# Two-layer hybrid trunk on one core: one more pair of feed-forward tiles with held weights, the normalised product one slot later, the last norm's sums one product later

## The chip, the cores and the metric

One core of a Trainium2 chip. The metric is the device time of one execution in microseconds. TensorE (PE) multiplies, VectorE (DVE) and ScalarE (ACT) work on what it leaves in PSUM and prepare its operands in SBUF, and the queue of SyncE (SP) issues nearly all DMAs. GpSimd (POOL) does next to nothing here.

## The reference

Input and output are 256 tokens by 1024 channels in float32. Layer 0 mixes tokens by a short gated convolution, layer 1 by block-sparse causal attention (with 256 tokens it is causal attention in one block, 16 heads of 64, rotary positions). After each comes the feed-forward that the change is about:

```python
def rmsnorm(x, g):
    var = jnp.mean(x * x, axis=-1, keepdims=True)
    return (x * lax.rsqrt(var + RMS_EPS)) * g

def conv_ffn(h, w_up, w_conv, w_down):          # w_up 1024 x 5632, w_down 2816 x 1024
    gu = causal_dwconv(h @ w_up, w_conv)        # three taps along the tokens
    g, u = jnp.split(gu, 2, axis=-1)
    return (jax.nn.silu(g) * u) @ w_down

for i in range(2):
    x = x + mixer_i(rmsnorm(x, mix_norm[i]))
    x = x + conv_ffn(rmsnorm(x, ffn_norm[i]), ffn_w_up[i], ffn_w_conv[i], ffn_w_down[i])
return rmsnorm(x, final_norm)
```

## The kernel before

**Numbers in two parts.** Every operand of PE is split into a high part `hi` (or `h`) and a rest `lo` (`l`), and a product is three matmuls: high by high, high by low, low by high. All weights come from HBM once, as 204 units of 128x1024, two units to a DMA of 1 MB (`raw<-wall`), four such buffers. For each unit ACT writes `hi<-raw` and DVE `lo<-raw,hi`. There are six buffers of each, so a unit is split up to six units before PE uses it.

**Order.** Each engine is wrapped in `InOrder`: it runs its instructions in the order in which the program writes them, and an instruction that waits holds back all behind it. `PLAN` lists the units in the order in which PE uses them. After each unit's matmuls `slot()` splits one more unit and then moves every task in `tasks` on by one piece; the tasks are Python generators, started by `spawn`, each `yield` ending a piece. So "a slot" is the time of one unit on PE.

**A feed-forward, `ffn(layer, ...)`.** 2816 features are 22 tiles of 128, each with a gate half and an up half. Tiles 2c and 2c+1 are pair c. A pair is computed in one of two ways.

- Pairs in `TURNED[layer]` go *wide*: four units `W c.kk` of 12 matmuls each, in which the input x is loaded as the stationary operand and the weights stream by, 512 columns at a time. The result lies by tokens in two PSUM banks (`w0_8_0` is layer 0, pair 8, tokens 0 to 127) and has to be turned. `crossed` does that: two DVE `STREAM_TRANSPOSE` into a buffer, then 16 small DMAs on SP's queue into a second buffer. The two buffers are both called `flip` in layer 0; in layer 1 the first is `vts` and the second `late`. `SETTLE` counts the slots from there until the task `whole` takes tile 2c (`SETTLE - 5` slots) and tile 2c+1 (one more). It also sets when `ffn_steps` thinks the tile ready to be used.
- The others go with *held weights*, by `narrow`: one unit per half and tile, the weights as the stationary operand, 8 times a matmul of 512 and one of 256 columns. The result lies by features; `gathered` adds its two parts (an ACT copy and a DVE add for each half).

`whole` then makes a tile into an operand: the product `gn` with 1/rms (`rstd`, DVE, 128x512), the three taps (`gy`: two ACT, four DVE instructions), silu (`s`, ACT), the product with the up half (`p`, DVE) and its split into `ps..h` (ACT) and `ps..l` (DVE). `ps_18l` in the profile is the low part of tile 18 (of either layer).

A *down* step `D j` multiplies tile j by its unit of `w_down` into accumulators `fo` (24 matmuls of 256 columns in layer 0, 12 of 512 in layer 1, where the result lies by tokens). `ffn_steps` puts a down step behind every second up step as soon as a tile is ready; the rest stand at the end, by readiness. The last two downs (layer 0) or three (layer 1) are done column by column in `acc.finish`, so that what follows can start early.

With the numbers of before, the end of layer 0's feed-forward is, in PE's order: W8.2 W8.3 D10 W9.0 W9.1 D11 W9.2 W9.3 D12, tile 20, D13, tile 21, D14 D15 D16 D17 D20 D18, and at the end D19 with D21. In layer 1: W9.0 W9.1 D12 W9.2 W9.3 D13, tile 20, D14, tile 21, D15 D16 D17 D20, and at the end D18, D19, D21.

**The norm.** The up-projection starts before the norm's sum is known, and 1/rms is applied to its result. `finish_norm` sums the squares over features by two matmuls with ones (`ss<-totalh`, `ss<-totall`) into a PSUM bank, ACT takes the square root (`rms`), DVE the reciprocal. `n` counts the steps of the loop in `ffn`; in layer 1 the first two (tile 0) are done ahead of the loop, so that n = 0 is the third product.

Of the kernel before, what the change touches and what calls it, by code (L numbers as in the profile page):

```python
# [55 lines left out]
FIRST += [(k, tuple((j, i) for j in range(2) for i in range(3))) for k in range(HALVED, ND)]  # L56


TURNED = {0: range(10), 1: range(1, 10)}
SETTLE = 6  # L60


def ffn_steps(layer):

    ups = []
    for c in range(NF // 2):
        if c in TURNED[layer]:
            ups += [("wide", layer, c, kk) for kk in range(4)]
# [3 lines left out]
    for i, key in enumerate(ups):  # L72
        steps.append(key)
        n += 1
        if key[0] == "wide" and key[3] == 3:
            ready.update({2 * key[2] + j: n + SETTLE + 5 + j for j in range(2)})
        elif key[:3] == ("up", layer, 1):
# [31 lines left out]
INDEX = {k: i for i, k in enumerate(PLAN)}  # L109
# [57 lines left out]
def trunk(ctx: ExitStack, tc: tile.TileContext, x, wall, small, ropes, masks, final, out):  # L167
# [21 lines left out]
    def line(pool, w, off=0, dtype=F32, **kw):  # L189

        return pool.tile([P, -(-(off + w) // LINE) * LINE], dtype, **kw)[:, off : off + w]
# [8 lines left out]
    def by_place(v):  # L200
        return v.rearrange("p (i a) -> p a i", a=2)
# [85 lines left out]
    def spawn(*gens):  # L287
        tasks.extend(gens)

    def slot(splits=1, ahead=True, order=None):  # L290

        def place(g):
            name = g.__name__
            if order:
                return (*order, name).index(name)
            return 2 * (name not in ("copied", "gathered")) + ((name == "rotate") == ahead)

        for _ in range(splits if ahead else 0):
            split_next()
        for g in sorted(tasks, key=place):  # L300
            if next(g, StopIteration) is StopIteration:
                tasks.remove(g)
        for _ in range(0 if ahead else splits):
            split_next()
# [83 lines left out]
    def table(func):  # L388

        t = line(ap_, 1, name="table", tag="table", bufs=1)  # L390
        S.activation(t, ones[:, 0:1], func)
# [186 lines left out]
    def split_act(h, l, v):  # L578
        S.activation(h, v, AF.Copy)
        V.tensor_sub(l, v, h.bitcast(F32))  # L580

    def half_tile(name):
        return ap_.tile([P, T], F32, name=name, tag="t", bufs=NT)

    def pair_tile(name):
        return ap_.tile([P, 2, T], F32, name=name, tag="big", bufs=NBIG)

    def split_turned(name, v):

        h, l = (turned(name=name + c, tag="ps" + c, bufs=NPS) for c in "hl")  # L590
        split_act(h.places, l.places, by_place(v))
        return h.columns, l.columns
# [175 lines left out]
    def ffn(layer, nm, i, then, turns):  # L768
        acc, ps = (TokenAccum if then is None else Accum)(f"fo{layer}"), {}
        gus = {}  # L770
        tag = "ab"[then is not None]

        gns = {}

        def gathered(j, h):

            t = gns[j][:, h, :].rearrange("p (a i) -> p a i", a=2)
            S.activation(t, by_place(gus[j][h][:, 1, :]), AF.Copy)
            V.tensor_add(t, by_place(gus[j][h][:, 0, :]), t)
            yield  # L780

        def whole(j, src=None, wait=0):
            for _ in range(wait):
                yield
            y = pair_tile(f"gy{layer}_{j}")
            s, p = half_tile(f"s{layer}_{j}"), half_tile(f"p{layer}_{j}")
            if src is None:
                gn = gns.pop(j)
                V.tensor_mul(gn, gn, nm.r[:, None, :].to_broadcast([P, 2, T]))
            else:  # L790
                gn = pair_tile(f"gn{layer}_{j}")
                V.tensor_mul(
                    gn.rearrange("p h (b i) -> p h b i", i=32),
                    src,
                    nm.r.rearrange("p (b i) -> p b i", i=32)[:, None].to_broadcast([P, 2, 8, 32]),
                )
            yield
            taps(*((y[:, h, :], gn[:, h, :], partial(ffn_tap, layer, half=h, j=j)) for h in range(2)))
            yield
            S.activation(s, y[:, 0, :], AF.Silu)  # L800
            V.tensor_mul(p, s, y[:, 1, :])
            yield
            if layer == 0:
                ps[j] = split_turned(f"ps{layer}_{j}", p)
                return
            ps[j] = split_tiles(f"ps{layer}_{j}", f"down{layer}")
            split_act(*ps[j], p)

        def crossed(c, banks):

            there, back = (v[c % 2] for v in turns)
            for t in range(2):
                V.transpose(there[:, t], banks[t])
            dst = back.rearrange("p (t b f) -> p t b f", t=2, b=4)
            for b in range(4):
                for q in range(4):
                    Q.dma_start(
                        dst[32 * q : 32 * q + 32, :, b],
                        there[32 * b : 32 * b + 32, :, q * P : (q + 1) * P],
                    )  # L820
                yield
            src = back.rearrange("p (b j h i) -> p j h b i", j=2, h=2, i=32)
            spawn(*(whole(2 * c + j, src[:, j], SETTLE - 5 + j) for j in range(2)))

        def wide(c, kk):
            if kk == 0:
                gus[c] = [
                    bank(f"w{layer}_{c}_{t}", tag=tag).rearrange("p a t -> p (a t)") for t in range(2)
                ]
            wh, wl = (  # L830
                w.rearrange("p (k a i) -> p k i a", k=2, a=2) for w in unit(("wide", layer, c, kk))
            )
            for k2 in range(2):
                k = 2 * kk + k2
                s = (slice(None), k2)
                for t in range(2):
                    xh, xl = (x_[:, t * P : (t + 1) * P] for x_ in nm.plain[k])
                    kw = {"skip_group_check": True}
                    E.matmul(gus[c][t], xh, wh[s], start=k == 0, stop=False, **kw)
                    E.matmul(gus[c][t], xl, wh[s], start=False, stop=False, **kw)  # L840
                    E.matmul(gus[c][t], xh, wl[s], start=False, stop=k == 7, **kw)
            if kk == 3:
                spawn(crossed(c, gus.pop(c)))

        def narrow(h, j):
            gu = bank(f"gu{layer}_{j}_{h}", tag=tag)
            if h == 0:
                gns[j] = pair_tile(f"gn{layer}_{j}")
                gus[j] = []
            gus[j].append(gu)  # L850
            project_both(gu, unit(("up", layer, h, j)), nm)
            spawn(gathered(j, h))
            if h and j:
                spawn(whole(j))

        steps = ffn_steps(layer)
        if ("up", layer, 0, 0) in steps:
            gus[0] = [bank(f"gu{layer}_0_{h}", tag=tag) for h in range(2)]
            gns[0] = pair_tile(f"gn{layer}_0")
            wg, wu = unit(("up", layer, 0, 0)), unit(("up", layer, 1, 0))  # L860
            for ks in ((0, 1), (2, 3), (4, 5), (6, 7)):
                project_both(gus[0][0], wg, nm, ks)
                project_both(gus[0][1], wu, nm, ks)
            spawn(gathered(0, 0), gathered(0, 1))
            steps = steps[2:]
            if then is None:
                spawn(turn(acc))
            slot(ahead=layer == 0)
            slot(ahead=layer == 0)
        else:  # L870
            assert then is not None
        last = 2 + (then is None)
        downs = [key for key in steps if key[0] == "down"]
        final = downs[-last:]
        for n, key in enumerate(steps[:-last]):
            if key[0] == "wide":
                wide(*key[2:])
            elif key[0] == "up":
                narrow(*key[2:])
            else:  # L880
                acc.add(key, ps[key[2]], key == downs[0], False)
            if layer == 0 and n == 4:
                Q.dma_start(rope, ropes)
                S.dma_start(mk, masks)
            if n == (2 if key[0] == "wide" and layer == 0 else 0):
                finish_norm(i, nm, tag=tag, ps=acc.b[3] if layer == 0 else None)
                if ("up", layer, 1, 0) in INDEX:
                    spawn(whole(0))
            if n == (3 if layer == 0 else 1):
                table(AF.Silu)  # L890
            slot(ahead=layer == 0 or n > 3 * LAG_FFN)
        while tasks:
            slot(0)
        table(AF.Sqrt)
        acc.finish(final, [ps[key[2]] for key in final], then)
# [451 lines left out]
```

## Time and profile before

| | |
|---|---|
| runs | 562.41, 562.59, 560.62 us (median 562.41) |
| profiled execution | 558.52 us, of which the span 556.7 |
| mean granted PE clock | 0.993 |
| busy of the span | PE 97%, DVE 89%, ACT 65% |
| chain that ended last | PE 88%, DVE 7%, DMA 2%, ACT 1%, issue 1% |
| transposes | 20 `flip<-w` and 18 `vts<-w` on DVE |
| small DMAs of `crossed` | 160 `flip<-flip` and 144 `late<-vts` of 32 KB, 3.4 us from issue to landing |
| wide matmuls | 608 `w<-hi,x` and 304 `w<-lo,x` of 512 columns, 379 ns |
| held matmuls | 96 `gu<-x,hi` of 512, 383 ns; 96 `gu<-x,lo` of 256, 273 ns |

Matmuls overlap: a matmul of 512 columns starts 0.22 us after the one before it, one of 256 columns 0.11, though each takes longer from start to end. A row of the timeline gives start, duration, engine, line, operation, what it writes and reads without buffer numbers, shapes, and in brackets for how long the engine was idle before it and what ended that. All lines are L150, the helper through which every instruction goes, so places are told apart by tiles and times.

### The profile page before, as it was taken

To read this page: it belongs to the slowest core of one execution; us is meant where nothing else is said; L and a number is where in the kernel's file an instruction comes from. 1 tells how busy PE (TensorE), PEld (TensorE's weight loads), DVE (VectorE), ACT (ScalarE), POOL (GpSimd) and SP (SyncE) were. 2 spreads that over 40 slices of the span, in tenths; PEclk is the share of its full clock that TensorE was granted. 3 is DMA by queue.
4 is the path that set the end of the run, shared out by engine and by line. 5 is a ranking of instruction groups with operands and counts; after the bars stand their busy time and mean duration, and the time that the engine had idled before them with its cause. 6 is when DMAs were issued, how large, how long until landed. Compare 5 with 4: busy or idle time off the path is not lost.

```text
span 556.7 us, 9269 instructions
## 1 busy us (share of the span) xinstructions
PE 540.9 (97%) x3319; PEld 491.0 (88%) x3319; DVE 496.9 (89%) x865; ACT 362.0 (65%) x628; POOL 7.9 (1%) x12
## 2 busy tenths in 40 slices
PE   9999999999999999996999999999999999999976
PEld 9999999888999999996989888898888888888965
DVE  6899998879988989999899999799969899999993
ACT  7656667555656656677757888876745566656654
POOL 0021010000000000000000000000000000000000
PEclk9999999999999999999999999999999999999998
DMA  8956774566767776765353444564757766666501
GB/s 278 380 191 227 258 266 152 208 195 215 233 230 239 253 259 239 247 231 184 121 214 154 152 152 164 215 226 153 272 189 244 275 244 220 235 240 238 187 3 75
DMA packets 43645, 117.76 MB, mean 212 GB/s; under 512 B 7120, under 2 KB 30032, under 8 KB 31568
## 3 DMA queue, kind: packets, MB, share of 16 engines
q1 hardware_dynamic: 43024, 116.44, 60.2%
q10 hardware_dynamic: 576, 0.74, 0.4%
q8 instruction: 26, 0.43, 0.3%
q14 instruction: 19, 0.16, 0.1%
HBM read 105.09 MB, written 1.05 MB: 191 GB/s over the span
## 4 chain that ended last, share of the span: by engine, by line
PE 88%; DVE 7%; DMA 2%; ACT 1%; issue 1%; SPq 0%; DVEq 0%; ACTq 0%
PE w L150 35%; PE fo L150 20%; PE v L150 6%; PE gu L150 4%; PE q L150 4%; PE mo L150 4%; PE k L150 4%; PE b L150 3%; DVE lo L150 3%; DMA raw<-wall 2%; PE cv L150 2%; PE c L150 2%; DVE gy L150 1%; PE s L150 1%; PE o L150 1%
## 5 line engine op out<-in xcount | busy, mean ns | idle before, releaser
L150 DVE TENSOR_TENSOR lo<-raw,hi 128x1024 fp32r<-128x1024 f32 (+3 forms) x204 | 239.6, 1187 | 15.5 <-ACT hi L150 14.7
L150 ACT ACTIVATE hi<-raw 128x1024 fp32r<-128x1024 f32 (+1 forms) x202 | 202.7, 1023 | 27.9 <-PE w L150 13.0
L150 PE MATMUL w<-hi,x 128*128 128x512 f32 x608 | 180.9, 379 | 0.0
L150 PEld LDWEIGHTS w<-hi,x 128*128 128x128 f32 x608 | 113.8, 189 | 15.5
L150 PE MATMUL w<-lo,x 128*128 128x512 f32 x304 | 115.2, 379 | 0.0
L150 DVE SCALAR_TENSOR_TENSOR gy<-gn,sm,gy 128x254 f32<-128x254 f32 (+1 forms) x176 | 73.1, 480 | 0.0
L150 ACT ACTIVATE gy<-gn,sm 128x256 f32<-128x256 f32 x88 | 39.8, 501 | 49.1 <-DVE gn L150 48.9
L150 PEld LDWEIGHTS w<-lo,x 128*128 128x128 f32 x304 | 57.5, 189 | 8.2
L150 ACT ACTIVATE s<-gy 128x256 f32<-128x256 f32 x44 | 18.3, 417 | 37.7 <-DVE gy L150 37.7
L150 PE MATMUL gu<-x,hi 128*128 128x512 f32 x96 | 31.9, 383 | 0.0
L150 PE MATMUL gu<-x,lo 128*128 128x256 f32 x96 | 26.2, 273 | 0.0
L150 PE MATMUL b<-x,hi 128*128 128x256 f32 (+1 forms) x96 | 25.2, 313 | 0.0
L150 DVE TENSOR_TENSOR gn<-flip,rstd 128x512 f32<-128x512 f32 x20 | 13.8, 689 | 12.4 <-DMA flip<-flip 11.9
L150 PE MATMUL cv<-x,hi 128*128 128x256 f32 x128 | 23.3, 281 | 0.0
L150 DVE TENSOR_TENSOR gn<-late,rstd 128x512 f32<-128x512 f32 x18 | 12.4, 690 | 11.1 <-DMA late<-vts 11.1
L150 PE MATMUL q<-x,hi 128*128 128x512 f32 x64 | 21.8, 389 | 0.0
L150 PE MATMUL ao<-ohl,hi 128*128 128x512 f32 x64 | 21.3, 385 | 0.0
L150 PE MATMUL k<-x,hi 128*128 128x512 f32 x64 | 21.2, 382 | 0.0
L150 PEld LDWEIGHTS gu<-x,hi 128*128 128x128 f32 x96 | 18.1, 189 | 2.6
L150 PEld LDWEIGHTS cv<-x,hi 128*128 128x128 f32 x128 | 20.0, 196 | 0.0
L150 PE MATMUL v<-hi,x 128*128 128x512 f32 x64 | 19.2, 382 | 0.0
L150 DVE TENSOR_TENSOR p<-s,gy 128x256 f32<-128x256 f32 x44 | 18.5, 421 | 0.0
(525 smaller groups left out, 1167.7 us busy)
## 6 DMA issues: line engine op xcount, KB each, us to landing
raw<-wall SPq DMA_DIRECT2D x94, 1024.0 KB, 5.3
flip<-flip SPq DMA_DIRECT2D x160, 32.0 KB, 3.4
late<-vts SPq DMA_DIRECT2D x144, 32.0 KB, 3.4
raw<-wall SPq DMA_DIRECT2D x9, 192.0 KB, 4.1
raw<-wall SPq DMA_DIRECT2D x3, 384.0 KB, 6.0
raw<-wall SPq DMA_DIRECT2D x2, 512.0 KB, 8.7
late<-vts SPq DMA_DIRECT2D x16, 64.0 KB, 2.0
out<-of SPq DMA_DIRECT2D x3, 256.0 KB, 2.1
```

The source lines that it names most:

```text
L150: r = f(*args, **kw)
```

## The change

```diff
 FIRST += [(k, tuple((j, i) for j in range(2) for i in range(3))) for k in range(HALVED, ND)]
 
 
-TURNED = {0: range(10), 1: range(1, 10)}
-SETTLE = 6
+TURNED = {0: range(9), 1: range(1, 9)}
+SETTLE = 7
 
 
...
@@ -850,8 +850,6 @@
             gus[j].append(gu)
             project_both(gu, unit(("up", layer, h, j)), nm)
             spawn(gathered(j, h))
-            if h and j:
-                spawn(whole(j))
 
         steps = ffn_steps(layer)
         if ("up", layer, 0, 0) in steps:
@@ -867,8 +865,6 @@
                 spawn(turn(acc))
             slot(ahead=layer == 0)
             slot(ahead=layer == 0)
-        else:
-            assert then is not None
         last = 2 + (then is None)
         downs = [key for key in steps if key[0] == "down"]
         final = downs[-last:]
@@ -882,12 +878,14 @@
             if layer == 0 and n == 4:
                 Q.dma_start(rope, ropes)
                 S.dma_start(mk, masks)
-            if n == (2 if key[0] == "wide" and layer == 0 else 0):
+            if n == 2 - layer:
                 finish_norm(i, nm, tag=tag, ps=acc.b[3] if layer == 0 else None)
-                if ("up", layer, 1, 0) in INDEX:
+                if layer == 1:
                     spawn(whole(0))
-            if n == (3 if layer == 0 else 1):
+            if n == 3 - 2 * layer:
                 table(AF.Silu)
+            if key[:3] == ("up", layer, 1):
+                spawn(whole(key[3]))
             slot(ahead=layer == 0 or n > 3 * LAG_FFN)
         while tasks:
             slot(0)

```

Pair 9 (tiles 18 and 19) leaves `TURNED` in both layers and goes with held weights. `SETTLE` starts `whole` of the remaining wide pairs one slot later. For held tiles `whole` is now started in the loop, ahead of that step's slot, as it was from `narrow`. `finish_norm` in layer 1 moves from the third product to the fourth (n = 0 to n = 1), and the spawn of tile 0 with it; in layer 0 it stays at n = 2. `table(AF.Silu)`, which loads ACT's table, stays at n = 3 and n = 1. Layer 0's branch without a held first tile loses an assertion only.

The end of layer 0's feed-forward becomes W8.2 W8.3 D10, tile 18, D11, tile 19, D12, tile 20, D13, tile 21, D14 D15 D18 D16 D17 D19, and at the end D20 with D21. In layer 1: D11, tile 18, D12, tile 19, D13, tile 20, D14, tile 21, D15 D18 D16 D17, and at the end D19, D20, D21.

Three places in the order of instructions follow; names carry the layer and the tile, then a running number of the buffer (`gn0_14` is layer 0's tile 14; `w0_8_0` pair 8).

DVE in layer 0 around the transposes of wide pair 8; `gn0_14` and `gn0_15` are the products of pair 7, `lo91` and on are weight splits. Before:

```order
L150 TENSOR_TENSOR lo90_2584<-raw42_2401,hi90_2583 128x1024
L150 TENSOR_TENSOR gn0_14_2590<-flip_1270,rstd1_1327 128x512
L150 STREAM_TRANSPOSE flip_1270<-w0_8_0_2461 128x512
L150 STREAM_TRANSPOSE flip_1270<-w0_8_1_2462 128x512
L150 TENSOR_TENSOR lo91_2623<-raw42_2401,hi91_2622 128x1024
L150 SCALAR_TENSOR_TENSOR gy0_14_2587<-gn0_14_2590,sm_71,gy0_14_2587 128x255 x2
L150 SCALAR_TENSOR_TENSOR gy0_14_2587<-gn0_14_2590,sm_71,gy0_14_2587 128x254 x2
L150 TENSOR_TENSOR gn0_15_2635<-flip_1270,rstd1_1327 128x512
L150 TENSOR_TENSOR lo92_2658<-raw43_2475,hi92_2657 128x1024
L150 TENSOR_TENSOR p0_14_2589<-s0_14_2588,gy0_14_2587 128x256
```

And now:

```order
L150 TENSOR_TENSOR lo90_2584<-raw42_2401,hi90_2583 128x1024
L150 STREAM_TRANSPOSE flip_1270<-w0_8_0_2450 128x512
L150 STREAM_TRANSPOSE flip_1270<-w0_8_1_2451 128x512
L150 TENSOR_TENSOR lo91_2618<-raw42_2401,hi91_2617 128x1024
L150 TENSOR_TENSOR gn0_14_2624<-flip_1270,rstd1_1327 128x512
L150 TENSOR_TENSOR lo92_2651<-raw43_2464,hi92_2650 128x1024
L150 TENSOR_TENSOR gn0_18_2631<-gu0_18_0_2630,gn0_18_2631 128x256
L150 SCALAR_TENSOR_TENSOR gy0_14_2621<-gn0_14_2624,sm_71,gy0_14_2621 128x255 x2
L150 SCALAR_TENSOR_TENSOR gy0_14_2621<-gn0_14_2624,sm_71,gy0_14_2621 128x254 x2
L150 TENSOR_TENSOR gn0_15_2665<-flip_1270,rstd1_1327 128x512
```

The product of tile 14 stood ahead of the transposes of pair 8 and now stands behind them and one split; between the products of tiles 14 and 15 there is now the add that gathers the gate half of tile 18.

DVE in layer 0 where tile 18 is finished. Before, near the end:

```order
L150 TENSOR_TENSOR p0_18_2993<-s0_18_2992,gy0_18_2991 128x256
L150 SCALAR_TENSOR_TENSOR gy0_19_3034<-gn0_19_3037,sm_71,gy0_19_3034 128x255 x2
L150 SCALAR_TENSOR_TENSOR gy0_19_3034<-gn0_19_3037,sm_71,gy0_19_3034 128x254 x2
L150 TENSOR_TENSOR p0_21_2998<-s0_21_2997,gy0_21_2996 128x256
L150 TENSOR_TENSOR lo105_3110<-raw49_2839,hi105_3109 128x1024
L150 TENSOR_TENSOR ps0_18l_3114<-p0_18_2993,ps0_18h_3113 128x256
L150 TENSOR_TENSOR p0_19_3036<-s0_19_3035,gy0_19_3034 128x256
L150 TENSOR_TENSOR ps0_21l_3120<-p0_21_2998,ps0_21h_3119 128x256
```

And now, ahead of the product of tile 16:

```order
L150 TENSOR_TENSOR p0_18_2708<-s0_18_2707,gy0_18_2706 128x256
L150 TENSOR_TENSOR lo96_2802<-raw45_2581,hi96_2801 128x1024
L150 TENSOR_TENSOR gn0_19_2753<-gu0_19_1_2782,gn0_19_2753 128x256
L150 TENSOR_TENSOR ps0_18l_2808<-p0_18_2708,ps0_18h_2807 128x256
L150 TENSOR_TENSOR gn0_19_2753<-gn0_19_2753,rstd1_1327 128x512
L150 TENSOR_TENSOR lo97_2840<-raw45_2581,hi97_2839 128x1024
L150 TENSOR_TENSOR gn0_16_2846<-flip_1270,rstd1_1327 128x512
```

The split of tile 18 (`ps0_18l`) was the third last of the feed-forward's DVE work; it now stands 38 rows ahead of the last, before the products of the last wide pair (`gn0_16` and 17).

PE in layer 1 around the sums of the last norm, `ss3`; `gu1_1_0` and `gu1_1_1` are the gate and up halves of tile 1. Before:

```order
L150 MATMUL gu1_1_0_4588<-x3_7_4501,hi140_4421 128x512
L150 MATMUL gu1_1_0_4588<-x3_7_4501,lo140_4422 128x256
L150 MATMUL ss3_4606<-totalh3_4520,ones_r_76 128x256
L150 MATMUL ss3_4606<-totall3_4521,ones_r_76 128x256
L150 MATMUL gu1_1_1_4633<-x3_0_4334,hi141_4447 128x512
L150 MATMUL gu1_1_1_4633<-x3_0_4334,lo141_4448 128x256
```

And now:

```order
L150 MATMUL gu1_1_1_4630<-x3_7_4509,hi141_4455 128x512
L150 MATMUL gu1_1_1_4630<-x3_7_4509,lo141_4456 128x256
L150 MATMUL ss3_4647<-totalh3_4528,ones_r_76 128x256
L150 MATMUL ss3_4647<-totall3_4529,ones_r_76 128x256
L150 MATMUL w1_1_0_4670<-hi142_4484,x3_0_4342 128x512 x2
L150 MATMUL w1_1_0_4670<-lo142_4485,x3_0_4342 128x512
L150 MATMUL w1_1_1_4671<-hi142_4484,x3_0_4342 128x512 x2
L150 MATMUL w1_1_1_4671<-lo142_4485,x3_0_4342 128x512
```

The two sums stood between the halves of tile 1 and stand now between its up half and the first wide pair, `w1_1`.

## The prediction

> **What bounds the kernel now.** I read the page's first section, then the chain of work that ended last, then the waits. The page:
>
> ```profile
> span 556.7 us, 9269 instructions
> PE 540.9 (97%) x3319; PEld 491.0 (88%) x3319; DVE 496.9 (89%) x865; ACT 362.0 (65%) x628; POOL 7.9 (1%) x12
> ```
>
> PE is busy for 97% of the span, so a gain must come from the few microseconds in which it waits or runs slowly. The profiled execution took 558.52 us, of which 1.8 lie around the span; the median of the runs, 562.41, is 3.9 above it. I make the sum in the profiled execution and take it off the median. About 0.5% (2.8 us) is what a measurement of this kernel can tell from no change.
>
> The chain, in order of time, around the ends of the two feed-forwards (start, us, what):
>
> ```profile
> 211.41 2.68 PE fo L150 x24
> 214.09 5.18 PE w L150 x24
> ...
> 229.81 5.24 PE gu L150 x32
> ...
> 242.97 13.41 PE fo L150 x120
> ...
> 256.92 1.13 DVE lo L150
> ...
> 261.35 0.43 DVE ps_18l L150
> ...
> 261.82 9.75 PE fo L150 x71
> ...
> 539.86 1.58 DVE gy L150 x4
> ```
>
> A down-projection (24 `fo` matmuls) costs 2.68 us, half a wide pair 5.18, a held tile 5.24. From 242.97 five downs run without a pause; then the chain leaves PE for DVE until `ps_18l`, the low half of tile 18's product. The waits (total, times, longest) and PE's own rows at both places say the same:
>
> ```profile
> PE fo L150 <- ACT ps_18h L150: 4.9, 2, 2.5
> PE fo L150 <- DVE ps_18l L150: 3.9, 2, 2.5
> DVE gn L150 <- DMA flip<-flip: 11.9, 8, 2.7
> DVE gn L150 <- DMA late<-vts: 11.1, 7, 3.6
> ```
>
> ```profile
> 256.09 0.28 PE L150 MATMUL fo<-ps_20h,lo 128*128 128x256 f32 x1
> 258.91 0.38 PE L150 MATMUL fo<-ps_18h,hi 128*128 128x256 f32 x1 [2.54 <-ACT ps_18h L150]
> 261.82 0.58 PE L150 MATMUL fo<-ps_18l,hi 128*128 128x256 f32 x1 [2.54 <-DVE ps_18l L150]
> ```
>
> ```profile
> 537.62 0.38 PE L150 MATMUL fo<-lo,ps_20h 128*128 128x512 f32 x1
> ...
> 540.36 0.48 PE L150 MATMUL fo<-hi,ps_18h 128*128 128x512 f32 x1 [2.36 <-ACT ps_18h L150]
> 542.16 0.79 PE L150 MATMUL fo<-hi,ps_18l 128*128 128x512 f32 x1 [1.32 <-DVE ps_18l L150]
> ...
> 545.16 0.38 PE L150 MATMUL fo<-lo,ps_19h 128*128 128x512 f32 x1
> ```
>
> PE is then slow for some 3 us. The clock by stretches (length, PE busy, granted clock, DMA share, GB/s), the last one around a short pause that comes up below:
>
> ```profile
> 542.00:543.00 1.00, 0.84 (x2) 0.50 0.00 0
> ...
> 545.00:546.00 1.00, 1.00 (x6) 0.99 0.00 0
> ...
> 381.00:382.20 1.20, 0.94 (x5) 1.00 0.92 389
> ```
>
> DVE is why tile 18 is late. Its rows in the first feed-forward:
>
> ```profile
> 217.56 0.69 DVE L150 TENSOR_TENSOR gn<-flip,rstd 128x512 f32<-128x512 f32 x1 [0.87 <-DMA flip<-flip]
> 218.16 1.31 DVE L150 STREAM_TRANSPOSE flip<-w 128x512 f32<-128x512 f32 x2
> ...
> 232.80 0.69 DVE L150 TENSOR_TENSOR gn<-flip,rstd 128x512 f32<-128x512 f32 x1 [1.28 <-DMA flip<-flip]
> ...
> 250.74 0.68 DVE L150 TENSOR_TENSOR gn<-flip,rstd 128x512 f32<-128x512 f32 x1
> ...
> 261.35 0.42 DVE L150 TENSOR_TENSOR ps_18l<-p,ps_18h 128x256 fp32r<-128x256 f32 x1
> ```
>
> The wide pair 8 is complete on PE at 211.41, but its transposes start at 218.16: they stand behind the product `gn` of pair 7, which waits for its small DMAs. Pair 9 loses as much again, its tile 18 is multiplied by 1/rms only at 250.74, and the split comes out 5 us after PE wants it. In the second feed-forward the same rows are 499.80 (a `gn` that waited 1.10 us for `late<-vts`), 500.41 for the transposes of pair 8, and 541.67 for `ps_18l`:
>
> ```profile
> 499.80 0.69 DVE L150 TENSOR_TENSOR gn<-late,rstd 128x512 f32<-128x512 f32 x1 [1.10 <-DMA late<-vts]
> 500.41 1.31 DVE L150 STREAM_TRANSPOSE vts<-w 128x512 f32<-128x512 f32 x2
> ...
> 541.67 0.43 DVE L150 TENSOR_TENSOR ps_18l<-p,ps_18h 128x256 fp32r<-128x256 f32 x1
> ```
>
> **The product a slot later.** It now stands behind the next pair's two transposes and one weight split. A pair's DMAs have landed 14.6 us after its transposes began (218.16 to 232.80). PE's period per pair is 2 halves and 2 downs, 15.72, and the product comes 1.23 (two transposes) and 1.13 (a split) behind the next transposes: 18.1 us after its own, 3.5 to spare. So DVE waits for PE and no longer for DMA, and has the idle to catch up:
>
> ```profile
> 133.00:230.00 97.00, 97.00 (x602) 89.25 (x601) 88.98 (x146) 59.57 (x93) 0.00 (x0) 1.00 0.71 240
> ```
>
> DVE (third figure) is busy 88.98 of 97 us, with 8.0 us idle against a lag of 6.7 us (211.41 to 218.16). I followed DVE's instructions in their new order, each at its distance to the next in the rows of before (the product 0.60, from 217.56 to 218.16; two transposes 1.23, four taps 1.58, a split 1.13, a 256-wide instruction 0.34) and none ahead of the PE, ACT or DMA work that feeds it. In this walk DVE stands at PE's pace by pair 7, and the transposes of pair 8 start at about 211.5. The downs' inputs of early tiles come some 1 us later than before; the first is wanted 2.9 us after my estimate of it, so that costs nothing unless the catch-up fails (a rival below).
>
> **Pair 9 held.** Per feed-forward it removes two transposes and 16 small DMAs and adds four ACT copies and four DVE adds:
>
> ```profile
> L150 DVE STREAM_TRANSPOSE flip<-w 128x512 f32<-128x512 f32 x20 | 13.1, 693 | 0.0
> L150 DVE TENSOR_TENSOR gn<-gu,gn 128x256 f32<-128x256 f32 x12 | 4.9, 415 | 0.0
> ```
>
> PE: two tiles at 5.24 for two halves at 5.18, +0.12 us on its path. DVE: four adds at 0.415 for two transposes at 0.693, +0.27; and since tiles 18 and 19 come ahead of 16 and 17 in the order, the stretch from pair 8's transposes to the last split holds 43.7 us of work instead of 42.7 (41.4 instead of 40.4 in the second). ACT's copies lie in its 35% of idle time, behind matmuls that PE has done. SP has 32 DMAs fewer; nothing waits on SP there.
>
> First feed-forward, from pair 8's end at 211.41: D10, tile 18, D11, tile 19, D12, tile 20, D13, tile 21, which is 4×2.68+4×5.24 = 31.7, to 243.1; six downs (14, 15, 18, 16, 17, 19) to 259.2; the last two, 5.4, to 264.5. Before it was 271.57 (261.82+9.75). The 7.15 us that were lost are two pauses of 2.7 and 2.8 and 1.65 of slow clock; minus 0.12 that is a gain of **7.0**, if DVE keeps up. My walk gives for tile 18 a split at 231 (wanted 248.4), for 16 at 245.0 (251.1), 17 at 248.7 (253.8), 19 at 242.9 (256.5), 21 at 257.2 (259.5: 211.5+43.7, and 2.0 of waiting for tile 21 from PE). Nothing stalls; the least slack is 2.3. The bounds are 7.0 and, with DVE no earlier than before, 4.6.
>
> Second feed-forward: what was lost there is 2.5 and 1.6 of pauses and 1.5 of slow clock (7 matmuls from 542.16 to 545.16 at twice their 0.216), 5.6 in all. After it PE wants tile 21 some 2.6 us into the end, where tile 19 leads: 537.84+0.12+2.59 = 540.55. My walk starts pair 8's transposes at 498.65, and DVE then does 41.4 us of work with 2.2 of waiting for PE: the high half of tile 21 at 541.85, the low at 542.33. That leaves pauses of about 1.2 and 0.25, with 0.3 of slack ahead of tile 17. Gain 5.6−0.12−1.45 = **4.0**; bounds 3.7 (transposes as late as before) and 5.5 (no pause). The tail behind PE, 551.44 to 556.7, has the same work.
>
> Does such a pause cost clock too? The row nearest to it is the pause of 0.26 us at 381.48 (its row is below), at clock 1.00 by the stretch above, where the two of 2.36 and 1.32 with one matmul between went to 0.50; I take no cost, and keep 1.5, the second's slow matmuls, as the upper end. [...]
>
> **The sums of the last norm.** They sit between two products:
>
> ```profile
> 380.95 0.27 PE L150 MATMUL gu<-x,lo 128*128 128x256 f32 x1
> 381.48 0.36 PE L150 MATMUL ss<-totalh,ones_r 128*128 128x256 f32 x1 [0.26 <-DVE totalh L150]
> 381.85 0.39 PE L150 MATMUL ss<-totall,ones_r 128*128 128x256 f32 x1
> 382.18 0.48 PE L150 MATMUL gu<-x,hi 128*128 128x512 f32 x1
> ```
>
> From 380.95 to 382.18 are 1.23 us where 0.11 is a matmul's own pace: 1.12 for two sums. Where nothing is late, two sums cost 0.24:
>
> ```profile
> 24.54 0.24 PE ss L150 x2
> ```
>
> A product (2.6 us) later `totalh` is long there. The next wide pair's second bank is the one the sums use, so it waits for ACT to read it: an estimated 0.1 (bounds 0 and 0.6). Gain 1.12−0.24−0.1 = **0.8** (0.3 to 0.9). 1/rms comes a product later on DVE; the first down there has some 10 us to spare by my walk, which hides it.
>
> **Sum:** 7.0+4.0+0.8 = 11.8: the profiled execution at 546.7, the median at 562.41−11.8 = 550.6.
>
> **The rivals.**
> 1. DVE does not catch up: the product still waits for its DMAs, only further down, and the transposes of pair 8 start as late as before. For it: DVE has 8.0 us of idle for a lag of 6.7, hardly more. Against: 3.5 us of room for the DMAs. Then tile 21 is ready at 218.16+43.7 = 261.9 against 259.5, 2.4 us lost, and 0.3 in the second: gain 9.1, 553.3; with the slow clock in both ends (1.65+1.5) 556.4.
> 2. All goes as forecast but the pause left in the second end halves the clock: 552.1.
> 3. No pause there, since a few of my 2.2 us of waiting aren't there: 549.1.
> 4. Slower: DVE becomes the bound. The added 1.05 us per feed-forward lies on the engine that is 89% busy, and copies and adds between the splits could hold it up. It decides where pair 8's transposes start 4.7 us later than before in the first (222.8, so that tile 21 comes 7.0 late). At 5.5 later in both, the first end loses 7.9+1.65+0.12−7.15 = 2.5, the second 7.3+1.5+0.12−5.6 = 3.3, the sums give 0.8: 567.4. Against: nothing ahead of pair 8 gains work, and the waits there are taken away.
> 5. No change to be told: the pauses only move to tiles 16, 17 and 21, with DVE some 3 to 4.5 us later than before: 560 to 564.
>
> **How the numbers follow.** As forecast 0.50; rival 1 0.18, rival 2 0.12, rival 3 0.11, rival 4 0.04, rival 5 0.05. The first four cases are faster by over 2.8 us: 0.91; same 0.05, slower 0.04. The predicted time is that of the likeliest, 550.6. The runs of before differ by 2.0 among themselves and the profiled one by 3.9 from the median, so each case carries about 1.5 either way: from rival 3's 549.1 less 1.5 to rival 1's 553.3 plus 1.5 and a part of its clock loss, 547.6 to 555.2, which leaves out rivals 4 and 5, the worst of 1 and the tails: 0.2.
>
> **What would show it.** Right: no `DVE gn <- DMA` waits in the list or hardly any; transposes of pair 8 within 1 us of PE's end of that pair in the first feed-forward; no row `PE fo <- ... ps_18`; the page's PE clock 1.00 around 260; the feed-forward's end 7 us nearer to that pair's end; one pause of 1 to 1.5 us at `ps_21h` and `ps_21l` near the end; the sums' two matmuls 0.1 apart. Wrong: `gn` still waiting for `flip`; pauses at `ps_16`, `ps_17` or `ps_19`; a clock of 0.50 after them; a stall at the sums' bank longer than 0.6. What would undo the forecast most cheaply is DVE: every microsecond beyond 2.3 by which it is late at pair 8 comes back one for one at the first end, and in the second at once.

## The result and the profile after

The changed kernel takes 548.02 us in the median (four runs, 546.63 to 550.32), before 562.50 (560.62 to 562.64). The ratio is 0.9754, 95% interval 0.9715 to 0.9794. The profiled execution took 548.28 us, its span 546.5, against 558.52 and 556.7. The page after:

```profile
span 546.5 us, 9303 instructions
PE 538.1 (98%) x3351; PEld 489.1 (89%) x3351; DVE 496.8 (91%) x869; ACT 365.0 (67%) x636; POOL 7.9 (1%) x12
```

DVE does the same work in 10 us less. The waits that were shown of before, and one that has grown (before it was 4.8 us in 8):

```profile
ACT hi L150 <- DMA raw<-wall: 15.1, 14, 3.0
DVE gn L150 <- DMA flip<-flip: 8.5, 6, 2.5
...
DVE gn L150 <- DMA late<-vts: 2.9, 2, 1.9
```

PE no longer waits for `ps_18`. DVE has the low half of tile 18 in layer 0 at 233.84 (before: 261.35), and PE starts its down at 247.49:

```profile
233.84 0.46 DVE L150 TENSOR_TENSOR ps_18l<-p,ps_18h 128x256 fp32r<-128x256 f32 x1
```

In layer 1 (`late`) DVE hardly waits for its small DMAs any more; in layer 0 (`flip`) most of the waiting is still there. PE's rows around its remaining pauses, two at the end of layer 0 and one at the end of layer 1:

```profile
250.41 0.28 PE L150 MATMUL fo<-ps_16l,hi 128*128 128x256 f32 x1
251.13 0.38 PE L150 MATMUL fo<-ps_16h,lo 128*128 128x256 f32 x1 [0.44 <-DVE lo L150]
```

```profile
259.38 0.30 PE L150 MATMUL fo<-ps_21h,hi 128*128 128x256 f32 x1
260.24 0.38 PE L150 MATMUL fo<-ps_21l,hi 128*128 128x256 f32 x1 [0.55 <-DVE ps_21l L150]
```

```profile
534.12 0.38 PE L150 MATMUL fo<-lo,ps_20h 128*128 128x512 f32 x1
535.42 0.48 PE L150 MATMUL fo<-hi,ps_21h 128*128 128x512 f32 x1 [0.93 <-ACT ps_21h L150]
535.88 0.48 PE L150 MATMUL fo<-hi,ps_21l 128*128 128x512 f32 x1
```

Beyond a matmul's own pace these are 0.60, 0.74 and 1.33 us, where there were 5.5 and 4.1. No slow clock follows (stretch, PE busy, granted clock, DMA share, GB/s):

```profile
262.00:265.00 3.00, 3.00 (x29) 1.00 0.94 385
536.00:538.00 2.00, 2.00 (x10) 1.00 0.00 0
```

The sums in layer 1 now cost PE next to nothing; from the last product's matmul to the first of the wide pair are 0.35 us, where 1.23 were:

```profile
378.16 0.27 PE L150 MATMUL gu<-x,lo 128*128 128x256 f32 x1
378.27 0.29 PE L150 MATMUL ss<-totalh,ones_r 128*128 128x256 f32 x1
378.39 0.28 PE L150 MATMUL ss<-totall,ones_r 128*128 128x256 f32 x1
378.51 0.59 PE L150 MATMUL w<-hi,x 128*128 128x512 f32 x2
```

From here on I use a table of stages, each the time between the first matmuls of two parts, read from PE's rows of each trace (us; "to its last product" ends at the last matmul of that product, the last two stages at PE's last matmul and at the span's end):

| stage | before | before again (a1) | after | after again (c4) | pair 9 alone (a2) | product later alone (a3) | sums alone (a4) | without sums (b4) |
|---|---|---|---|---|---|---|---|---|
| up to layer 0's feed-forward | 90.96 | 90.21 | 90.17 | 90.17 | 90.52 | 90.65 | 90.42 | 90.89 |
| layer 0's feed-forward | 180.45 | 182.16 | 175.36 | 176.62 | 177.50 | 181.57 | 183.68 | 177.78 |
| attention | 101.79 | 101.80 | 102.25 | 102.26 | 102.25 | 101.80 | 101.80 | 102.29 |
| layer 1's tiles 0 and 1, sums | 11.70 | 11.70 | 10.72 | 10.72 | 11.70 | 11.70 | 10.72 | 11.71 |
| to its first down | 20.72 | 20.72 | 20.91 | 20.90 | 20.72 | 20.72 | 20.90 | 20.72 |
| to its last product | 121.74 | 121.74 | 121.86 | 121.86 | 121.86 | 121.74 | 121.74 | 121.86 |
| to PE's end | 24.07 | 25.47 | 19.91 | 21.26 | 20.90 | 25.87 | 26.01 | 21.30 |
| behind PE | 5.30 | 5.31 | 5.31 | 5.30 | 5.30 | 5.30 | 5.31 | 5.33 |

Nearly all of the 10.2 us between the first and third columns of numbers lie in the two feed-forwards' ends (5.1 and 4.2) and the sums (1.0).

### The profile page after: what moved, and what is told of

Its sections match the earlier page's. It is cut to its first block, busy times and chain, and to the rows that moved or that the text cites. A ratio compares the mean times of both kernels' runs of the same rounds, so it can differ in the third digit from the quotient of the medians.

```text
span 546.5 us, 9303 instructions
## 1 busy us (share of the span) xinstructions
PE 538.1 (98%) x3351; PEld 489.1 (89%) x3351; DVE 496.8 (91%) x869; ACT 365.0 (67%) x636; POOL 7.9 (1%) x12
## 4 chain that ended last, share of the span: by engine, by line
PE 66%; DVE 15%; DMA 13%; issue 3%; ACT 1%; SPq 1%; DVEq 0%; ACTq 0%
PE w L150 20%; DMA raw<-wall 11%; PE fo L150 8%; PE v L150 6%; DVE lo L150 6%; DVE gy L150 5%; PE cv L150 4%; PE q L150 4%; PE mo L150 4%; PE b L150 4%; PE ao L150 4%; PE k L150 4%; PE gu L150 2%; DVE gn L150 2%; PE c L150 2%
## 5 line engine op out<-in xcount | busy, mean ns | idle before, releaser
L150 ACT ACTIVATE hi<-raw 128x1024 fp32r<-128x1024 f32 (+1 forms) x202 | 203.8, 1024 | 55.4 <-PE w L150 25.4
L150 PE MATMUL w<-hi,x 128*128 128x512 f32 x544 | 161.9, 379 | 0.0
L150 PEld LDWEIGHTS w<-hi,x 128*128 128x128 f32 x544 | 101.8, 189 | 14.2 <-ACT rms L150 0.3
L150 PE MATMUL w<-lo,x 128*128 128x512 f32 x272 | 103.1, 379 | 0.0
L150 PEld LDWEIGHTS w<-lo,x 128*128 128x128 f32 x272 | 51.4, 189 | 7.2
L150 PE MATMUL gu<-x,hi 128*128 128x512 f32 x160 | 52.9, 382 | 0.0
L150 PE MATMUL gu<-x,lo 128*128 128x256 f32 x160 | 43.6, 273 | 0.0
L150 PEld LDWEIGHTS gu<-x,hi 128*128 128x128 f32 x160 | 30.3, 189 | 4.1
L150 ACT ACTIVATE s<-gy 128x256 f32<-128x256 f32 x44 | 18.3, 416 | 23.3 <-DVE gy L150 23.2
L150 PEld LDWEIGHTS gu<-x,lo 128*128 128x128 f32 x160 | 30.7, 192 | 0.1
L150 PE MATMUL ao<-ohl,hi 128*128 128x512 f32 x64 | 21.3, 385 | 0.0
L150 DVE TENSOR_TENSOR gn<-flip,rstd 128x512 f32<-128x512 f32 x18 | 12.4, 688 | 8.5 <-DMA flip<-flip 8.5
L150 PE MATMUL v<-hi,x 128*128 128x512 f32 x64 | 19.2, 382 | 0.0
```

Of the source, the lines that this page charges most:

```text
L150: r = f(*args, **kw)
```

## The experiments

**The kernel before, a second time.** No edit.

> The kernel before, unchanged, profiled a second time: the runs' medians lie 14.5 us apart, the two profiled executions only 10.2. Theory: the profiled execution of before (558.52 us) was one of its shorter ones; this one takes 560.6 to 562.6 us, its span is 558.8 to 560.8, and the 2 to 4 us more stand in the trace as longer pauses of PE, at the ends of the feed-forwards or at the start. Rival: the difference lies outside the span; then the span is 556.7 again and 4 to 6 us lie around it.

Measured 561.90 us (ten runs, 560.27 to 564.56), span 559.1. The theory holds, but pauses are not all of it. The 2.4 us over the first profile are layer 0's feed-forward (+1.7) and the last part (+1.4), less 0.75 at the start. PE's rows show longer pauses at the same places, 0.4 us more in layer 0 and 1.4 in layer 1:

```profile
258.56 0.38 PE L150 MATMUL fo<-ps_18h,hi 128*128 128x256 f32 x1 [2.95 <-ACT ps_18h L150]
261.48 0.58 PE L150 MATMUL fo<-ps_18l,hi 128*128 128x256 f32 x1 [2.54 <-DVE ps_18l L150]
```

```profile
542.69 0.48 PE L150 MATMUL fo<-hi,ps_18h 128*128 128x512 f32 x1 [3.73 <-ACT ps_18h L150]
544.49 0.80 PE L150 MATMUL fo<-hi,ps_18l 128*128 128x512 f32 x1 [1.32 <-DVE ps_18l L150]
```

The other 1.3 us in layer 0 are the clock. It stands at 0.50 from 260.7 to 267.5 in this trace, twice as long as in the first profile (261.7 to 265.1):

```profile
266.00:267.00 1.00, 1.00 (x7) 0.50 0.63 246
```

So how late tile 18 comes, and how long the clock stays down behind it, differ from execution to execution (the 25 runs of before that shared this chip reach from 557.3 to 565.2 us), and the profile on which the forecast rests caught a short one. From this profile to that of after it is 12.6 us of span, not 10.2.

**Pair 9 alone.**

```diff
-SETTLE = 7
+SETTLE = 6
-            if n == 2 - layer:
+            if n == 2 - 2 * layer:
```

(against the changed kernel)

> Only pair 9 goes with held weights; the product's slot (SETTLE 6) and the place of the norm's sums stay as before. Theory (the new place of tiles 18 and 19 in the order carries the gain): about 554 us, 8 less than before; transposes of pair 8 start as late as before (6 to 7 us behind PE in layer 0), no pause at tile 18, a pause of 2 to 3 us at tile 21 in layer 0 and of 1.5 to 2 us in layer 1, no slow clock. Rival (the later product carries it): 560 us or more, with pauses over 2 us at tile 18 or 16.

Measured 551.52 us, ratio 0.9827 (0.9791 to 0.9862). The theory holds, the rival is out: this part alone brings some 10 us. DVE waits for the small DMAs about as long as before (11.9 and 11.1 us there), and pair 8's transposes start 8.6 us behind PE's end of that pair in layer 0, later than before (6.9):

```profile
DVE gn L150 <- DMA flip<-flip: 12.8, 8, 2.9
DVE gn L150 <- DMA late<-vts: 10.6, 7, 2.6
```

So the gain does not come from shorter waits ahead of pair 8. What is left is that tiles 18 and 19 are finished earlier in DVE's order; no run gives them that place without also changing how they are multiplied. The pauses are not where the theory had them:

```profile
244.12 0.38 PE L150 MATMUL fo<-ps_14h,lo 128*128 128x256 f32 x1 [1.26 <-DVE lo L150]
...
247.84 0.38 PE L150 MATMUL fo<-ps_15h,lo 128*128 128x256 f32 x1 [0.77 <-DVE lo L150]
...
262.73 0.38 PE L150 MATMUL fo<-ps_21l,hi 128*128 128x256 f32 x1 [0.22 <-DVE ps_21l L150]
```

In layer 0 PE waits first for `lo`, the low half of the down's own weights: the weight splits stand in the same line on DVE as the products, and are due earlier. Those early pauses give the tiles behind them time. In layer 1 the pause at tile 21 is 2.32 us (2.08 and 0.24).

**The product later, alone.**

```diff
-SETTLE = 6
+SETTLE = 7
```

(against the kernel before)

> Only SETTLE 7: the product a slot later, pair 9 stays wide, the sums stay. Theory: transposes of pair 8 start some 3 us earlier than before in layer 0 and up to 6 us earlier in layer 1, but tile 18 stays last in line and its product comes a slot (2.7 us) later there, so the pauses at tile 18 stay: 559 to 564 us. Rival (waiting for the small DMAs was the cause of the late tile 18): both pauses fall below 2 us and the slow clock goes, 552 us or less.

Measured 561.48 us, ratio 1.0016 (0.9982 to 1.0050): no gain. Pair 8's transposes start 4.3 us behind PE's end of that pair in layer 0 and 2.2 in layer 1 (6.9 and 4.1 before), and DVE waits 9.2 and 2.9 us for small DMAs instead of 11.9 and 11.1, much as in the changed kernel. But tile 18 is still last in line, and its own product is a slot later:

```profile
259.93 0.58 PE L150 MATMUL fo<-ps_18h,hi 128*128 128x256 f32 x1 [3.88 <-ACT ps_18h L150]
262.57 0.58 PE L150 MATMUL fo<-ps_18l,hi 128*128 128x256 f32 x1 [2.06 <-DVE ps_18l L150]
```

**The sums alone.**

```diff
-            if n == (2 if key[0] == "wide" and layer == 0 else 0):
+            if n == 2 - layer:
```

(against the kernel before)

> Only the last norm's sums behind the fourth product. Theory: the stretch from the first product of layer 1's feed-forward to its first wide pair is 1.0 us shorter, and the time falls by 0.8 at most. Rival: the second end is set by DVE, which is busy without a break there, so that PE waits there for what it saved here: the stretch is 1.0 shorter, the pause at tile 18 in layer 1 as much longer, and the time is that of before.

Measured 561.03 us, ratio 1.0012 (0.9983 to 1.0041). The stretch is 0.98 us shorter, and the time is that of before. The profiled execution has the last part at 26.01 where the one of a1 has 25.47, so that 0.5 of the gain is seen to come back there; with tile 18's lateness as scattered as a1 shows, one trace doesn't prove the rest. The runs lean to the rival but don't exclude the theory's 0.8: their interval reaches from 1.0 us less to 2.3 more.

**The changed kernel without the sums.** The same line as in a2, with SETTLE 7.

> The changed kernel with the sums back behind the third product. Theory (alone the sums gained nothing because DVE set the second end; with pair 9 held, PE's own work sets it but for 1.3 us): the stretch to the first wide pair is 1.0 us longer, the pause at tile 21 shorter by some of it, time 548.4 to 548.9. Rival (DVE still sets the end): the pause shrinks by the whole 1.0, 548.0.

Measured 550.21 us, ratio 0.9757 (0.9724 to 0.9791), against 0.9754 (0.9715 to 0.9794) with them. Nothing to be told apart: with pair 9 held, too, the sums' place brings no time that these runs could show. The step from a2's 0.9827 to this 0.9757 is the later product: some 0.7% (intervals that just touch), with pair 9 held, where it brought nothing alone. No trace shows where: the spans of the two profiled executions are 550.8 (a2) and 551.9 us.

**Four last downs.**

```diff
-        last = 2 + (then is None)
+        last = 2 + 2 * (then is None)
```

> The changed kernel, with four downs instead of three taken column by column at the end of layer 1, so that tile 21 is first used 1.3 us later. Theory (PE's pause of 1.33 us there is only tile 21 coming late, and what follows has no other bound): the pause falls to 0.1 us or less, the last part after the last product is 1.2 us shorter, 546.8 us. Rival (what is saved is lost behind PE, in ACT's and DVE's norm of the first 128 tokens, which now comes 1.3 us later): 548.

Measured 549.38 us, ratio 0.9762. The edit did the opposite of what I meant: a whole down takes 2.6 us and its half in the last part 1.3, so tile 21 is wanted 1.3 us earlier, and the pause doubled:

```profile
535.23 0.48 PE L150 MATMUL fo<-hi,ps_21h 128*128 128x512 f32 x1 [2.22 <-ACT ps_21h L150]
```

PE's last part grew by 1.3, to 21.22.

**Two last downs.**

```diff
-        last = 2 + (then is None)
+        last = 2
```

> The changed kernel, with two downs instead of three taken column by column at the end of layer 1. A whole down lasts 2.6 us and its first half 1.3, so with four of them tile 21 came 1.3 us earlier, not later, and its pause grew from 1.33 to 2.62; with two it is wanted 1.3 us later. Theory (the pause is only tile 21 coming late): it falls to 0.1 us or less, the part from the last product to PE's end is 18.6 us instead of 19.9, the time 546.7. Rival (the norm of the first 128 tokens comes later and the work behind PE grows): 548.

Measured 549.57 us, ratio 0.9766 (0.9738 to 0.9795). The pause is gone but for 0.24, PE's last part is 18.81 us instead of 19.91, and the part behind PE 6.62 instead of 5.31: the rival holds. The chain that ended last no longer goes through PE there:

```profile
537.48 0.42 ACT ps_21h L150
537.91 1.28 ACT L150
539.20 0.20 ACT table L150
539.41 0.27 ACT end L150
539.68 0.12 ACT sq L150
```

Behind the high half of tile 21 (`ps_21h`) ACT loads its table for the square root (the row of 1.28 us, ACT_TABLE_LOAD in ACT's timeline) and then squares the first 128 tokens. In the changed kernel ACT does the same from 534.96 on, and the table loads at 535.39 while PE multiplies tile 21. From the start of `ps_21h` to the span's end are 11.5 us in both traces. So the end waits for tile 21 either way, and the pause costs nothing: from the last product to the span's end are 25.2 us with it and 25.4 without.

**The changed kernel again.** No edit.

> The changed kernel again, for comparison on this chip: 548 us, with pauses of 0.6 and 0.7 us in layer 0 and 1.3 in layer 1.

Measured 548.87 us, ratio 0.9750 (0.9720 to 0.9781). The profiled execution was its longest (550.88), with two pauses more, again at a weight's low half in layer 0 and at `ps_17l` in layer 1:

```profile
249.00 0.38 PE L150 MATMUL fo<-ps_18h,lo 128*128 128x256 f32 x1 [1.12 <-DVE lo L150]
```

**Loads from POOL's queue.** In the changed kernel's trace no DMA of SP's queue is issued before the one eight places ahead has landed (none of 409, where 91 are issued before the one seven places ahead has; one is issued at 116.36, when the load eight places ahead has landed at 116.34), so I suspected SP's queue.

```diff
         elif queue is None:
-            load_part(Q, c, 0, w)
+            load_part(G if PLAN[CHUNKS[c][0]][0] in ("wide", "up", "down") else Q, c, 0, w)
```

> The changed kernel, with the weight loads of the feed-forwards issued from POOL's queue; SP's queue keeps the small DMAs. In the changed kernel every DMA of SP's queue waits for the landing of the one eight places ahead of it, so a small DMA often waits for a load of 1 MB. Theory (that wait is what still holds the products of layer 0 back, 8.5 us in all): DVE's waits for small DMAs fall below 2 us, pair 8's transposes start within 1.5 us of PE's end of that pair, both pauses in layer 0 (0.6 and 0.7 us) go, its feed-forward takes 173.5 to 174.2 us instead of 175.4, and the time is 546 to 547 us. Rival (the loads and the small DMAs share the same 16 engines, busy 66%, and land late for that): the waits stay above 6 us and the time at 548. Third: loads issued from POOL come later, splits wait for them, 550 us or more.

Measured 558.33 us, ratio 0.9917 (0.9885 to 0.9950): a clear loss, and none of the three foresaw how. The loads don't come late (ACT waits 4.0 us for them, not 15.1). The small DMAs do, once in each layer, at the first pair:

```profile
DVE gn L150 <- DMA late<-vts: 7.9, 1, 7.9
...
DVE gn L150 <- DMA flip<-flip: 6.3, 1, 6.3
```

PE runs out of tiles at once, at downs 0 and 2, and the clock follows:

```profile
134.55 0.38 PE L150 MATMUL fo<-ps_0l,hi 128*128 128x256 f32 x1 [2.13 <-DVE ps_0l L150]
```

```profile
135.00:136.00 1.00, 1.00 (x7) 0.50 0.98 400
136.00:137.00 1.00, 1.00 (x6) 0.50 0.75 212
137.00:138.00 1.00, 1.00 (x7) 0.50 1.28 158
```

After that no product waits for a small DMA, and layer 0 ends without a pause; but PE has by then lost more than the ends can give back (layer 0's feed-forward 177.83 us, layer 1 to its last product 129.05).

**Loads from POOL's queue from pair 3 on, and with two last downs.**

```diff
         elif queue is None:
-            load_part(Q, c, 0, w)
+            u = CHUNKS[c][0]
+            late = PLAN[u][0] in ("wide", "up", "down") and u >= INDEX["wide", PLAN[u][1], 3, 0]
+            load_part(G if late else Q, c, 0, w)
```

> As b1_loads_on_pool, but the loads go from POOL's queue only from wide pair 3 on, since that kernel waited 6.3 and 7.9 us for the first pair's small DMAs and for none after them. Theory (in the middle of a feed-forward the small DMAs are held back by the loads ahead of them on SP's queue): no long wait at the first pairs, waits of DVE for small DMAs in layer 0 below 3 us in all, pair 8's transposes within 1.5 us of PE, no pause at the end of layer 0, 173.5 to 174 us for that feed-forward, and 0.4 less in the attention after it: 546 us. Rival (two streams of transfers hold each other up wherever the second begins): a wait of over 5 us moves to pair 3 or 4, and the time is 548 or more.

> c1 and c2 together. Theory: their gains add, 544.7 us. Rival: one of them takes the other's place, 546 or more.

Measured 558.28 us (0.9917) and 555.64 (0.9882). Both theories fall, and so does the first one's rival, which had the wait at pair 3 or 4, though its time came. Loads are issued up to eight units ahead of their splits, so pair 3's are already under way when the first pair's small DMAs are issued, and the waits stand where they stood:

```profile
DVE gn L150 <- DMA flip<-flip: 7.5, 2, 6.1
DVE gn L150 <- DMA late<-vts: 7.4, 1, 7.4
```

These traces show what the small DMAs land behind. Issue and landing around the first pair, from the DMA records (us):

```
changed kernel (all on SP's queue)        loads on POOL's queue from pair 3 on (c2)
DMA        issued  landed                 DMA              issued  landed
flip       109.39  111.28                 load (POOL)      106.72  112.36
flip       110.04  111.91                 flip             106.76  112.43
load 1 MB  110.74  116.34                 flip             107.40  112.62
flip       111.30  116.52                 rope 384 KB      108.04  115.37
flip       111.93  116.69                 flip             108.68  116.74
flip       112.96  116.86                 load (POOL)      109.11  116.57
flip       113.60  117.07                 flip             109.31  116.92
flip       114.24  117.23                 flip             109.95  117.09
```

In these rows a small DMA with no load ahead lands in 1.9 us (109.39 to 111.28). One that is issued behind a load lands 0.1 to 0.4 us after that load, and the next ones at steps of 0.2, and this is so when the load was issued from another queue (c2's flips of 106.76 and 109.31). At the first pair, changing the queue therefore doesn't let them pass; it lets more loads be under way at once (in b1 five are issued between 98 and 115 us, three in the changed kernel). At later pairs, behind PE's first pauses, the small DMAs do come sooner: those of pairs 7 and 8 of layer 0 land 15.7 and 16.4 us after their transposes in b1, 19.7 and 19.2 in the changed kernel.

## Why the prediction was right, and where its steps were not

The time (548.0 for 550.6), the sign and the chief cause hold: tile 18's place in the order ended its pauses and the slow clock behind them. That the time came so near is in part luck: in layer 0 DVE caught up by only 2.1 of its 6.9 us, which is for the most part rival 1's mechanism, and the gain between the profiles, 10.2, lies between rival 1's 9.1 and the forecast's 11.8. By the steps:

- **Pair 9 held, layer 0: 7.0, measured 5.1** between the two profiled executions, and 0.5 of that is given back in the attention (102.25 for 101.79), where DVE comes late with the next norm's input; a1 as the base makes it 6.8. Layer 0's program is the same in before, a1 and a4 (180.45, 182.16, 183.69) and in the changed kernel, b2, b4, c1 and c4 (175.24 to 177.78); in the mean of these traces the gain is 5.6. The term was near its lower bound, 4.6, as rival 1 has it. What failed in it is the step ahead, DVE's catch-up.
- **The product a slot later: "DVE waits for PE and no longer for DMA" was wrong in layer 0.** The waits fell from 11.9 to 8.5 us only. Pair 8's transposes start 4.8 us behind PE's end of that pair (6.9 before), not at once:

```profile
203.76 0.69 DVE L150 TENSOR_TENSOR gn<-flip,rstd 128x512 f32<-128x512 f32 x1 [2.50 <-DMA flip<-flip]
...
215.26 1.31 DVE L150 STREAM_TRANSPOSE flip<-w 128x512 f32<-128x512 f32 x2
```

```profile
210.46 0.27 PE L150 MATMUL fo<-ps_10h,hi 128*128 128x256 f32 x1
```

I had taken the landing of a pair's DMAs, 14.6 us after its transposes, for a fixed delay. It is not one, and this is the step that failed: the last of pair 7's DMAs lands 19.7 us after its transposes (198.85 to 218.53), that of pair 8 after 19.2, so the 3.5 us to spare were gone. The slot does this, not pair 9: a2, with the old slot, has 14.5 and 14.6, a3, with the new slot alone, 19.7 and 18.9. Counted from PE's end of the pair the landings hardly move, 23.6 and 23.2 us in a2, 23.1 and 23.2 in a3, 23.8 and 24.0 in the changed kernel, where the transposes start 9.2 and 8.6, 3.4 and 4.3, 4.1 and 4.8 us behind that end (other traces scatter from 21.3, before, to 26.2, b4). Transposes that start earlier do not make the DMAs land earlier. The chain that ended last now runs through the loads of layer 0:

```profile
202.90 7.57 DMA raw<-wall
...
210.48 0.59 SPq L150
...
211.16 5.47 DMA raw<-wall
...
216.65 1.88 DMA flip<-flip
...
218.59 0.57 issue
```

The load of 202.90 lands at 210.47; SP, which waits for it with a small DMA eight places behind, goes on at 210.48 and issues the next load, and the small DMAs land behind that one. A pair passes two such rounds, 15.7 us in these rows, which is PE's own period. So a slot's more time for the product would be little help: it covers a delay, and this looks like a rate that the loads set. That reading is not shown. It rests on the chain and on the landings above; whatever keeps step with PE repeats at PE's period, and moving the loads (b1, c2) changed the first pairs as well. With SETTLE 8, one slot more, the program no longer computes the two layers, so that its time (554.71 us) can't decide it. In layer 1 the step held for pair 8: transposes 2.0 us behind PE (490.23 to 492.28). The waits there, 2.9 us in this trace, are 7.1 in c4, whose program is the same, and its transposes of pair 8 stand as near to PE.
- **"Nothing stalls" in layer 0 was wrong by 0.60 and 0.74.** The deadlines I listed were those of products. The first pause is for the low half of a down's weights, which I didn't walk against its own deadline; the second is `ps_21l`, as rival 1 named it.
- **Second end: 4.0, measured 4.2.** The pause at tile 21 was forecast at 1.45 and is 1.33. Rival 2 is out, the clock stays at 1.00; but c1 shows that rival 3 wouldn't have given its 1.5 us either, since the work behind tile 21 takes as long without the pause.
- **The sums: the stretch came as forecast, 0.98 less and 0.19 back at the bank. As a term of the sum it was not shown:** alone (a4) and taken out (b4) it doesn't move the time by anything that the runs could tell. The likely reason, not shown by itself, is that the ends wait for DVE and ACT and not for PE.
- **The base.** The sum was made from a profile with shorter pauses than most executions of before have. Between the two profiled executions the gain is 10.2, so the steps gave 1.6 too much; between the medians it is 14.5, 4.3 more than between the profiles. The two errors have opposite signs, and the forecast is 2.7 short of the medians' gain instead of 4.3. That they partly cancel is luck.

Rivals 4 (DVE as the bound) and 5 (no change) fall with the result, though c1 and b4 show that the ends do hang on DVE and ACT.

## What to carry to other kernels

When a tile comes late to the end of a phase, look first at its place in the order of the engine that prepares it: moving tiles 18 and 19 ahead brought 10 us, while shortening the waits in front of a tile that stays last, and is a slot later for it, brought nothing. Before a wait for a DMA is booked as gone because there is more time for it, see what the DMA lands behind, and whether its landing moves when its issue does: more time is sure to help only against a fixed delay, and the landing here was none (pair 7's came 14.5 us behind its transposes in a2 and 19.7 in the changed kernel). A pause of PE is worth something only if nothing else needs that time (in c1 it fell from 1.33 us to 0.24, and from the last product to the span's end were 25.4 us, where the changed kernel has 25.2); and the gain should be worked out from more than one profiled execution where the runs of before scatter by 1%.

## What the runs showed of the hardware

Small transfers were seen to wait for large ones across queues: in c2, 32 KB issued on SP's queue 0.2 us after a 1 MB load from POOL's (109.31 and 109.11) landed 0.35 us after that load, 7.6 us after its own issue, where 1.9 us is what a small DMA took in the changed kernel with no load ahead (109.39 to 111.28). What holds it back no run here shows.

The clock fell to 0.50 behind one pause and not behind another that was as long. In b1 PE was idle for 2.13 us, with one matmul and 0.15 us of idle time ahead of it, and 3 us at 0.50 followed; in b2 a pause of 2.22 us after steady work left it at 1.00. In the clock records of before the granted clock is 0.50 from 261.71 to 265.12 and from 541.60 to 545.01, 3.41 us each time, at two pauses each (2.54 and 2.54 us, 2.36 and 1.32). In the 3.41 us ahead of these two falls PE is busy for 11% and 14% by its rows, in as long a stretch ahead of b1's first fall (134.78) for 33%. A stretch of 3.41 us busy for 43% (in before, from 254.9) was not followed by a fall. So in these traces the length of a single pause doesn't tell whether the clock falls. That it is how empty PE is over some microseconds is my reading of these few stretches; no run moves a pause to try it.
